# Two of six top-k selections moved behind the first blocks of the next attention head, with working tiles from that head's softmax ring

## The chip, the core and the metric

The kernel runs on one core of a Trainium2 chip. The metric is the device time of one execution in microseconds (us), the median of three runs where a median is given. The engines are called PE (matrix multiply, with PEld for its weight loads), DVE (the vector engine), ACT (the scalar engine), POOL (GpSimd) and SP, whose queue issues most of the DMA transfers. PSUM is the memory into which PE writes; a PSUM bank here holds a tile of 128x512 float32.

## What is computed

One decoder block on a sequence of 1024 rows and 1024 columns. After a projection, two attentions run side by side: eight "FoX" heads with a forget-gate bias, and eight "DSA" heads which see, for each query row, only the 256 keys with the highest indexer score, with a relative-position bias. The core of the second:

```python
iscore = jnp.where(causal[None], iscore, -jnp.inf)
_, sel = lax.top_k(iscore, topk)          # 256 of the keys s <= t
...
logits = logits + bias                     # relative-position bias
p = jax.nn.softmax(logits, axis=-1)
```

Gates, an output projection, a squared-ReLU MLP and a final norm follow. All matrix products are made from a high and a low part of each operand, three products for one.

## The kernel before

Rows are worked on in eight tiles of 128 query rows (i = 0 to 7). Row tile i sees (i + 1) * 128 keys, so the later tiles are the wider ones. Tiles 0 and 1 need no top-k.

**Selection.** The indexer scores of the tiles 2 to 7 stand in `isc` as sortable integers. A bisection over 32 bits (`bisect_step`, four steps for each FoX head) finds the threshold of each row. Then `select_tile(i)` (L521 to L535) makes the mask of tile i: nine DVE operations over (i + 1) * 128 columns and a read-back of one sum. They use two working tiles, `bjunk` (named gt) and `eqt` (named eq), of which there is one each, read `isc[i]`, and write the mask over `sel[i]`. The six calls stand at the end of the last FoX head's turn (L749 to L751).

**Attention.** `attention(kind, h, ...)` (L538) runs through four blocks qb = 0 to 3 of two row tiles each. For each row tile PE makes the scores S in PSUM (three banks go round, tag "S"), DVE adds the relative bias where there is one (L562) and adds the mask, taking the row minimum, into a softmax tile `sp` (L563), ACT makes the exponential (L567) and scales it (L570). Then PE transposes both tiles (L583), ACT and DVE split the transposes into `ph` and `pl` (L584, L585), and PE multiplies with V (pv). `sp` tiles come from a ring of four (tag "sp", bufs 4), two for each block. A DSA head's row tile i reads `sel[i]` from i = 2 on, so tiles 6 and 7 are read first in block qb = 3.

**Work beside it.** After each head's attention the program states the projection of the next head (`proj_qk`: two halves, each 24 matmuls of 128x512 into a PSUM bank of tag "g", of which there are two, emptied by ACT at L313 to L324 and by DVE at L318 and L325), for every second head `proj_v` (L338, L343, L344), gate tiles (`gate_tile`: two halves into the same "g" banks, emptied by ACT at L609), and, from the last FoX head on, `ada_later`, a chain of products on POOL (L618 to L627). These are PE's cover while the softmax chain of a head is under way.

**What sets the order.** The order on each engine is not the program's. A scheduler goes through a simulated timeline: an engine that is free takes, of the instructions whose inputs are there, the one that is stated first in the program. Rings of tiles go round in the order in which the program asks for tiles. On the chip every engine then goes through its list in that order, and waits where an input is late.

SP issues the loads for `branch_fox`, which go into the memory of `isc` (L649) after its last reader.

Of the kernel before, what the change touches and what calls it, by code (L numbers as in the profile page):

```python
# [11 lines left out]
BF16 = mybir.dt.bfloat16  # L12
# [9 lines left out]
P = 128  # L22
D = 1024
S = 1024
KT = D // P
NTT = S // P
# [31 lines left out]
def block_kernel(ctx: ExitStack, tc: tile.TileContext, x, c, w_ada, b_ada, g_norm1, w_in, b_forget,  # L58
# [5 lines left out]
    def pool(stack, name, bufs=1, **kw):  # L64
        if kw.get("space") != DRAM:
            kw.setdefault("reuse_waits", "tile")
        return stack.enter_context(tc.tile_pool(name=name, bufs=bufs, **kw))
# [260 lines left out]
    def proj_v(kind, pr):  # L328
        cv = (C_VF if kind == 0 else C_VD) + pr * P
        hi, lo = split_w([(0, P, win[:, :, cv:cv + P])], nc.gpsimd)  # L330
        V = [pQ.tile([P, NTT, P], F32R, name="V", tag="V", bufs=3) for _ in range(2)]
        for half in range(2):
            ps = gemm_h(hi, lo, half)
            vT = pQ.tile([P, 512], F32, name="t512", tag="t512", bufs=3)
            nc.scalar.activation(vT, ps, AF.Copy)
            tp = ptr.tile([P, 512], F32, name="vtr", tag="tr")
            for t in range(4):
                nc.tensor.transpose(tp[:, t * P:(t + 1) * P], vT[:, t * P:(t + 1) * P], ident)  # L338
            tv = tp.rearrange("p (t c) -> p t c", t=4)
            ts4 = slice(half * 4, half * 4 + 4)  # L340
            for s in range(2):
                src = tv[:, :, 64 * s:64 * s + 64]
                nc.scalar.activation(V[s][:, ts4, 0:64], src, AF.Copy)  # L343
                nc.vector.tensor_tensor(V[s][:, ts4, 64:128], src, V[s][:, ts4, 0:64].bitcast(F32), op=ALU.subtract)  # L344
        return V
# [114 lines left out]
    pA = pool(at_stack, "pA")  # L460
# [8 lines left out]
    bjunk = pA.tile([P, S], BF16, name="bjunk")  # L469
    eqt = pA.tile([P, S], BF16, name="eqt")  # L470
# [30 lines left out]
    def bisect_mid():  # L501
        nc.vector.tensor_scalar(cand, Thi, 1.0, None, op0=ALU.add)
        count(I16, cand)
        nc.vector.tensor_scalar(need, cnt, -1.0, float(TOPK), op0=ALU.mult, op1=ALU.add)
        for i in on_act:
            q = slice(i - 2, i - 1)
            nc.vector.tensor_scalar(need[:, q], cnt[:, q], -0.5, float(TOPK - (i + 1) * P // 2), op0=ALU.mult, op1=ALU.add)
        set_goal()
        for i in range(2, NTT):
            nc.vector.scalar_tensor_tensor(sel[i].bitcast(U16), sel[i].bitcast(I16), Thi[:, i - 2:i - 1],  # L510
                                           isc[i].bitcast(U16)[:, 0::2], op0=ALU.is_equal, op1=ALU.mult)
# [6 lines left out]
        nc.vector.tensor_tensor(cnt, cnt, goal, op=ALU.is_ge)  # L518
        nc.vector.scalar_tensor_tensor(T, cnt, v, T, op0=ALU.mult, op1=ALU.add)

    def select_tile(i):  # L521
        q, W = i - 2, (i + 1) * P
        hi = isc[i].bitcast(I16)[:, 1::2]
        L = sel[i].bitcast(U16)
        th, tl, nd = Thi[:, q:q + 1], Tlo[:, q:q + 1], need[:, q:q + 1]
        gt, eq = bjunk[:, :W], eqt[:, :W]
        nc.vector.tensor_scalar(gt, L, tl, None, op0=ALU.is_gt, op1=ALU.add, accum_out=cnt[:, q:q + 1])
        nc.vector.tensor_tensor(nd, nd, cnt[:, q:q + 1], op=ALU.subtract)
        nc.vector.tensor_scalar(eq, L, tl, None, op0=ALU.is_equal)
        nc.vector.scalar_tensor_tensor(gt, hi, th, gt, op0=ALU.is_gt, op1=ALU.add)  # L530
        nc.vector.scalar_tensor_tensor(eq, hi, th, eq, op0=ALU.is_equal, op1=ALU.mult)
        nc.vector.tensor_tensor_scan(out=L, data0=eq, data1=eq, initial=0.0, op0=ALU.add, op1=ALU.max)
        nc.vector.scalar_tensor_tensor(eq, L, nd, eq, op0=ALU.is_le, op1=ALU.mult)
        nc.vector.tensor_tensor(gt, gt, eq, op=ALU.add)
        nc.vector.tensor_scalar(sel[i], gt, -BIG, BIG, op0=ALU.mult, op1=ALU.add)  # L535


    def attention(kind, h, qk, V, Yd=None):  # L538
# [6 lines left out]
        for qb in range(NTT // 2):  # L545
            pt = []
            for s in range(2):
                i = 2 * qb + s
                W = (i + 1) * P
                qs = slice(i * P, (i + 1) * P)  # L550
                mn = pA.tile([P, 8], F32, name="mn", tag="mn", bufs=5)
                sp = pA.tile([P, S], F32, name="sp", tag="sp", bufs=4)
# [38 lines left out]
            nc.scalar.activation(yt, pv[64:128, :], AF.Copy)  # L591
            nc.vector.tensor_tensor(yt, pv[0:64, :], yt, op=ALU.add)  # L592
            nc.scalar.activation(yh, yt, AF.Copy)
            if (kind, h) == (1, NH - 1):
                cols = slice(qb * 256, (qb + 1) * 256)
                nc.scalar.activation(Yd[0][yr, 3, cols], yt, AF.Copy)
                nc.vector.tensor_tensor(Yd[1][yr, 3, cols], yt, yh.bitcast(F32), op=ALU.subtract)
                continue
# [4 lines left out]
    def gate_tile(g):  # L603
        col = (C_GF if g < 8 else C_GD) + (g % 8) * P
        hi, lo = split_w([(0, P, win[:, :, col:col + P])], nc.gpsimd)
        for half in range(2):
            ps = gemm_h(hi, lo, half)
            e = pQ.tile([P, 512], F32, name="t512", tag="t512", bufs=3)
            nc.scalar.activation(e, ps, AF.Tanh, scale=0.5)  # L609
            nc.sync.dma_start(G_d[g, :, half * 512:half * 512 + 512], e)  # L610
# [118 lines left out]
    for n, (kind, h) in enumerate(heads):  # L729
        qk = qk_next  # L730
        on_pool[0] = n < NH
        if h % 2 == 0:
            V = V_next
        attention(kind, h, qk, V[h % 2], Yd)
        if n + 1 < len(heads):
            qk_next = proj_qk(*heads[n + 1])
        if h % 2 == 1 and n + 1 < len(heads):
            V_next = proj_v(heads[n + 1][0], heads[n + 1][1] // 2)
        for g in GATES.get(n, ()):
            gate_tile(g)  # L740
        if n < NH:
            for b in range(4):
                if bit == 15:
                    bisect_mid()
                bisect_step(bit)
                bit -= 1
        if NH <= n + 1 < 2 * NH:
            ada_later(n + 1 - NH)
        if n == NH - 1:  # L749
            for i in range(2, NTT):  # L750
                select_tile(i)  # L751
        if n == 3:
            dsa_consts()
        for piece in PIECES.get(n, ()):
            branch_fox(piece)
        if n == 2 * NH - 2:
            h_stack.close()
            pYd = pool(yd_stack, "pYd", side="right")
            Yd = [pYd.tile([P, 4, S], F32R, name=f"Yd{v}") for v in range(2)]
            pY = pool(yd_stack, "pY", side="right")  # L760
# [14 lines left out]
    for half in range(2):  # L775
        sl = slice(half * 512, half * 512 + 512)
        for cp in range(4):
            hi, lo = split_w([(0, 256, wbv[1][:, :, cp * 256:cp * 256 + 256])], nc.gpsimd, 4)
            hv, lv = hi.rearrange("p (k c) -> p k c", k=4), lo.rearrange("p (k c) -> p k c", k=4)
            for c2 in range(2):  # L780
                ct, cs = 2 * cp + c2, slice(c2 * P, c2 * P + P)
                gt = pY.tile([P, 512], F32, name="gt2", tag="gt2", bufs=3)
# [432 lines left out]
```

## Time and profile before

| | us |
|---|---|
| median of three runs | 1624.54 |
| lowest and highest of them | 1622.43, 1626.76 |
| time of the profiled execution | 1624.31 |
| its span, first to last instruction | 1622.4 |
| PE busy | 1561.0 |
| DVE busy | 1142.8 |
| ACT busy | 946.8 |
| POOL busy | 742.1 |

The profiled execution stands 0.2 us under the median, and 1.9 us of its time lie outside the span. PE is busy for 96% of the span, so a change matters where it changes the idle time of PE, or the speed at which PE is clocked. The bisection ends at about 428 us, FoX head 6 runs to about 484, FoX head 7 from there to about 530 and the first DSA head from 514 to about 565; the heads overlap.

### The profile page before, as it was taken

The numbers are of one execution on the slowest core, as the hardware profiler recorded it, in microseconds if no ns is written. First come the engines' busy times: TensorE is split into PE (matmuls) and PEld (weight loads), VectorE is DVE, ScalarE is ACT, GpSimd is POOL, SyncE is SP. The second block draws the span as 40 slices with busy tenths as digits, with TensorE's granted clock in tenths as the row PEclk, the third lists the DMA queues.
The fourth block names the chain that finished last, engine by engine and source line by source line (L and its number), as shares of the span: only waits on it lengthen the run. The fifth ranks groups of instructions, "written<-read, shape, count | busy, mean of one in ns | idle before, by whom it ended". The sixth has DMA issues, their size and how long they took to land.

```text
span 1622.4 us, 22879 instructions
## 1 busy us (share of the span) xinstructions
PE 1561.0 (96%) x7585; PEld 1297.5 (80%) x7585; DVE 1142.8 (70%) x2230; ACT 946.8 (58%) x1689; POOL 742.1 (46%) x628
## 2 busy tenths in 40 slices
PE   5989999999989999999999998999999999999998
PEld 3767788887778888888887887888888878888887
DVE  6887778878897655557667546765655556668987
ACT  4455899898747767577763136554545543534433
POOL 3432222333234674756645211777776544334730
PEclk7999999999999999999999999999999999999999
DMA  9222122132124443544888456454444479755862
GB/s 307 78 47 60 52 80 57 44 79 50 53 63 140 119 139 99 153 135 138 300 262 272 144 164 225 150 161 162 149 147 160 164 263 388 244 201 199 280 208 104
DMA packets 223869, 253.01 MB, mean 156 GB/s; under 512 B 49136, under 2 KB 136256, under 8 KB 223752
## 3 DMA queue, kind: packets, MB, share of 16 engines
q1 hardware_dynamic: 215112, 233.73, 45.8%
q10 hardware_dynamic: 8640, 17.83, 2.9%
q8 instruction: 60, 0.98, 0.2%
q14 instruction: 57, 0.47, 0.1%
HBM read 186.48 MB, written 65.03 MB: 155 GB/s over the span
## 4 chain that ended last, share of the span: by engine, by line
PE 69%; DVE 10%; ACT 9%; issue 4%; DMA 4%; POOL 2%; SPq 1%; ACTq 0%; DVEq 0%; POOLq 0%
PE g L75 29%; PE S L75 23%; PE tr L75 8%; PE pv L75 7%; ACT eqt L495 4%; PE ptr L583 2%; DVE acc L252 2%; ACT sp L567 1%; ACT sp L570 1%; ACT ph L584 1%; DMA wap<-in_w_ada_dram 1%; DVE pl L585 1%; DMA gt<-G_d 1%; DVE sp L563 1%; DVE isc L434 1%
## 5 line engine op out<-in xcount | busy, mean ns | idle before, releaser
L75 PE MATMUL g<-h_hi,whi 128*128 128x512 f32 x656 | 263.8, 402 | 9.8 <-DVE KA L325 7.0
L75 PE MATMUL g<-h_hi,wlo 128*128 128x512 f32 x656 | 262.5, 400 | 0.0
L75 PE MATMUL g<-h_lo,whi 128*128 128x512 f32 x656 | 262.1, 399 | 0.0
L1036 DVE TENSOR_TENSOR big<-rw,big 128x1024 fp32r<-128x1024 f32 x112 | 174.7, 1605 | 76.7 <-ACT big L1035 76.7
L123 POOL TENSOR_TENSOR wlo<-st,whi 128x1024 fp32r<-128x1024 f32 x60 | 149.0, 2485 | 114.2 <-ACT whi L122 107.2
L1035 ACT ACTIVATE big<-rw 128x1024 fp32r<-128x1024 f32 x112 | 112.5, 1052 | 146.9 <-PE pv L75 63.2
L1051 POOL TENSOR_TENSOR rw<-rw 128x1024 f32<-128x1024 f32 x40 | 114.5, 2866 | 121.4 <-DMA rw<-in_w_mlp_dram 103.7
L75 PEld LDWEIGHTS g<-h_hi,whi 128*128 128x128 f32 x656 | 124.8, 190 | 35.5 <-issue 7.1
L75 PEld LDWEIGHTS g<-h_hi,wlo 128*128 128x128 f32 x656 | 124.4, 190 | 24.3
L75 PEld LDWEIGHTS g<-h_lo,whi 128*128 128x128 f32 x656 | 124.5, 190 | 22.7
L75 PE MATMUL S<-big 128*128 128x512 f32 (+1 forms) x576 | 136.5, 380 | 1.3 <-ACT big L1035 1.3
L75 PEld LDWEIGHTS S<-big 128*128 128x128 f32 x576 | 105.2, 188 | 22.3 <-ACT big L1035 1.7
L585 DVE TENSOR_TENSOR pl<-ptr,ph 128x512 fp32r<-128x512 f32 (+1 forms) x160 | 99.7, 631 | 23.7 <-ACT ph L584 20.6
L567 ACT ACTIVATE sp<-sp,mn 128x128 f32<-128x128 f32 (+7 forms) x128 | 98.5, 771 | 27.5 <-DVE mn L563 27.2
L584 ACT ACTIVATE ph<-ptr 128x512 fp32r<-128x512 f32 (+1 forms) x160 | 86.4, 550 | 43.6 <-PE ptr L583 41.7
L495 ACT ACTIVATE eqt<-sel_all,nct 128x768 bf16<-128x768 int16 (+5 forms) x99 | 102.5, 1035 | 10.0 <-DVE nct L491 8.7
L570 ACT ACTIVATE sp<-sp,mn 128x128 f32<-128x128 f32 (+7 forms) x128 | 96.9, 769 | 17.1 <-DVE mn L569 16.5
L75 PE MATMUL g<-big 128*128 128x512 f32 (+1 forms) x384 | 92.7, 376 | 0.0
L583 PE MATMUL ptr<-ident,sp 128*128 128x128 f32 x576 | 89.8, 272 | 1.7 <-DVE nct L491 1.2
L122 ACT ACTIVATE whi<-st 128x1024 fp32r<-128x1024 f32 x51 | 53.8, 1055 | 61.9 <-DMA st<-in_w_mlp_dram 19.4
L75 PE MATMUL pv<-ph,V 128*128 128x256 f32 x320 | 85.4, 286 | 3.1 <-DVE yt L592 3.1
L75 PE MATMUL pv<-pl,V 128*128 128x256 f32 x320 | 82.4, 285 | 2.8 <-DVE pl L585 1.6
(436 smaller groups left out, 3907.5 us busy)
## 6 DMA issues: line engine op xcount, KB each, us to landing
rw<-in_w_mlp_dram SPq DMA_DIRECT2D x72, 512.0 KB
rw<-U_d SPq DMA_DIRECT2D x56, 512.0 KB
wap<-in_w_ada_dram SPq DMA_DIRECT2D x64, 256.0 KB
st<-in_w_mlp_dram SPq DMA_DIRECT2D x32, 512.0 KB
st<-in_w_in_dram SPq DMA_DIRECT2D x26, 512.0 KB
U_d<-cc SPq DMA_DIRECT2D x48, 256.0 KB
st<-in_w_in_dram SPq DMA_DIRECT2D x33, 256.0 KB
G_d<-t SPq DMA_DIRECT2D x32, 256.0 KB
```

Source lines behind the costliest of these rows:

```text
L75: nc.tensor.matmul(o, l, r, start=start, stop=stop)
L122: nc.scalar.activation(hi, st, AF.Copy)
L123: (lo_eng or nc.vector).tensor_tensor(lo, st, hi.bitcast(F32), op=ALU.subtract)
L495: nc.scalar.activation(eqt[:, :(i + 1) * P], sel[i].bitcast(dt), AF.Sign, bias=nct[:, q], accum_out=cnt[:, q])
L567: nc.scalar.activation(sp[:, :W], sp[:, :W], AF.Exp, bias=mn[:, len(cs) - 1:len(cs)], scale=-1.0, accum_out=mn[:, 2:3])
L570: nc.scalar.activation(sp[:, :W], sp[:, :W], AF.Copy, scale=mn[:, 3:4])
L583: nc.tensor.transpose(tr[:, n * P:(n + 1) * P], pt[s][:, kb * P:(kb + 1) * P], ident)
L584: nc.scalar.activation(ph[:, z:], tr[:, z:], AF.Copy)
L585: nc.vector.tensor_tensor(pl[:, z:], tr[:, z:], ph[:, z:].bitcast(F32), op=ALU.subtract)
L1035: nc.scalar.activation(hl[:, 0], t, AF.Copy)
L1036: nc.vector.tensor_tensor(hl[:, 1], t, hl[:, 0].bitcast(F32), op=ALU.subtract)
L1051: nc.gpsimd.tensor_tensor(o, a, b, op=op)
```

## The change

`select_tile` takes an optional tile `room`, whose two halves replace `bjunk` and `eqt`. The calls for i = 6 and i = 7, the two widest, leave the last FoX head's turn. They are made inside the attention of the first DSA head (kind 1, h 0), after block qb = 0 (i = 6) and after block qb = 1 (i = 7), each with a `room` tile of the tag "sp", so that it takes one place of the ring of four.

```diff
-    def select_tile(i):
+    def select_tile(i, room=None):
...
-        gt, eq = bjunk[:, :W], eqt[:, :W]
+        gt, eq = (bjunk[:, :W], eqt[:, :W]) if room is None else (room[:, :W], room[:, S:S + W])
...
             nc.scalar.activation(yh, yt, AF.Copy)
+            if (kind, h) == (1, 0) and qb < 2:
+                room = pA.tile([P, 2 * S], BF16, name="room", tag="sp", bufs=4)
+                select_tile(6 + qb, room)
...
-            for i in range(2, NTT):
+            for i in range(2, 6):
                 select_tile(i)
```

## Rows read from the trace of the kernel before

**Rows 1.** Windows of 10 us: length, busy by engine (instructions), PE clock, DMA.

```profile
470.00:480.00 10.00, 7.05 (x23) 5.20 (x23) 9.94 (x14) 4.28 (x9) 8.05 (x5) 0.83 0.03 7
490.00:500.00 10.00, 10.00 (x57) 8.56 (x56) 9.96 (x15) 5.18 (x11) 3.43 (x5) 1.00 0.62 200
...
530.00:540.00 10.00, 10.00 (x55) 8.56 (x54) 5.39 (x15) 6.12 (x15) 4.57 (x8) 1.00 0.66 170
540.00:550.00 10.00, 10.00 (x55) 8.40 (x54) 6.27 (x20) 6.83 (x13) 6.03 (x6) 1.00 0.26 79
```

**Rows 2.** Timeline of PE: start, duration, instruction [idle before, releaser].

```profile
445.74 0.47 PE L75 MATMUL g<-h_hi,whi 128*128 128x512 f32 x1 [2.60 <-DVE KA L325]
...
473.21 0.35 PE L75 MATMUL pv<-ph,V 128*128 128x256 f32 x1 [1.61 <-DVE yt L592]
474.90 0.51 PE L75 MATMUL g<-h_hi,whi 128*128 128x512 f32 x1 [1.34 <-DVE KA L325]
475.25 0.40 PE L75 MATMUL g<-h_lo,whi 128*128 128x512 f32 x1
475.48 0.59 PE L75 MATMUL g<-h_hi,wlo 128*128 128x512 f32 x1
...
478.85 0.43 PE L75 MATMUL g<-h_lo,whi 128*128 128x512 f32 x1
```

**Rows 3.** Timeline of DVE, end of tile 6 and tile 7's selection.

```profile
483.11 0.39 DVE L535 TENSOR_SCALAR sel_all<-bjunk 128x896 bf16<-128x896 bf16 x1
483.42 0.48 DVE L529 TENSOR_SCALAR eqt<-sel_all,Tlo 128x1024 bf16<-128x1024 uint16 x1
...
484.49 1.28 DVE L527 TENSOR_SCALAR_CACHE_REDUCE bjunk<-sel_all,Tlo 128x1024 bf16<-128x1024 uint16 x1
...
489.35 2.27 DVE L532 TENSOR_TENSOR_SCAN sel_all<-eqt 128x1024 uint16<-128x1024 bf16 x1
...
493.79 0.67 DVE L534 TENSOR_TENSOR bjunk<-bjunk,eqt 128x1024 bf16<-128x1024 bf16 x1
...
495.32 3.19 DVE L535 TENSOR_SCALAR sel_all<-bjunk 128x1024 bf16<-128x1024 bf16 x1
```

**Rows 4.** Timeline of ACT at the two stalls of PE.

```profile
470.43 0.38 ACT L591 ACTIVATE yt<-pv 64x256 f32<-64x256 f32 x1
470.84 0.60 ACT L320 ACTIVATE KA<-g 64x512 fp32r<-64x512 f32 x1
```

**Rows 5.** Timeline of DVE, then PE: the ring of softmax tiles, first DSA head.

```profile
530.06 0.56 DVE L563 CUSTOM_DVE_ANT_0 sp<-S,sel_all 128x384 f32<-128x384 f32 x1 [0.32 <-PE ptr L583]
...
541.21 0.56 DVE L563 CUSTOM_DVE_ANT_0 sp<-S,sel_all 128x384 f32<-128x384 f32 x1 [3.09 <-PE ptr L583]
...
548.00 0.69 DVE L563 CUSTOM_DVE_ANT_0 sp<-S,sel_all 128x512 f32<-128x512 f32 x1 [0.25 <-PE ptr L583]
...
540.79 0.49 PE L583 MATMUL ptr<-ident,sp 128*128 128x128 f32 x3
```

**Rows 6.** Timelines of ACT, DVE, PE: the banks of PE's cover, same head.

```profile
529.65 0.60 ACT L324 ACTIVATE KB<-g 64x512 fp32r<-64x512 f32 x1
...
531.27 0.69 DVE L325 TENSOR_TENSOR KA<-g,KA 64x512 fp32r<-64x512 f32 x1
...
535.18 0.39 PE L75 MATMUL g<-h_hi,whi 128*128 128x512 f32 x1
...
553.18 0.59 ACT L313 ACTIVATE QA<-g 64x512 fp32r<-64x512 f32 x1 [0.85 <-PE S L75]
```

**Rows 7.** Windows of 30 us, columns as Rows 1; then one POOL instruction.

```profile
469.00:499.00 30.00, 27.05 (x132) 22.55 (x133) 29.77 (x45) 13.55 (x28) 12.61 (x13) 0.94 0.30 82
520.00:550.00 30.00, 30.00 (x168) 25.84 (x167) 17.78 (x46) 20.98 (x45) 19.37 (x21) 1.00 0.49 138
...
494.80 2.85 POOL L123 TENSOR_TENSOR wlo<-st,whi 128x1024 fp32r<-128x1024 f32 x1 [5.17 <-DMA isc<-Y_d]
```

**Rows 8.** Waits of SP's queue, 425 to 600 us: total, times, longest.

```profile
SPq L649 <- DVE mn L569: 7.6, 1, 7.6
```

## The prediction

> **What bounds the kernel now.** I read the page's busy times first (the table above): PE is by far the busiest, so only its idle time and its clock can give anything back. Next come the windows over the stretch that the change touches [rows 1]. Between 470 and 480 us PE is busy for 7.05 of 10 us, at a mean granted clock of 0.83, and DVE is full (9.94). Between 490 and 500 DVE is still full, and PE is full as well: there PE has other work. From 530 to 550, in the first DSA head, PE is full and DVE has 4.6 and 3.7 us free in 10.
>
> The timeline of PE names what it waits for [rows 2]. Two waits lie where tiles 6 and 7 are selected: 1.61 us for yt (L592) and 1.34 us for KA (L325), both on DVE. After them comes a slow piece: eight matmuls from 475.48 to 478.85 take 3.37 us, 0.42 each, while the pair from 475.25 to 475.48 is 0.23 apart. PE had stood still for most of the 3.5 us ahead of 474.90, and then ran at the lower of its two levels (1.2 instead of 2.4 GHz). The earlier wait of 2.60 us at 445.74 belongs to the tiles before tile 6, which stay where they are and are ordered before anything that moves, so it stays.
>
> **What the change removes.** *The work.* Tile 7's selection [rows 3]: L529 0.48, then four operations over 1024 columns of about 1.28 each (L527 stands for them, the others are L530, L531, L533), the scan 2.27, L534 0.67, L535 3.19. Two short ones are left out. L535 of tile 6, over 896 columns, took 0.39, so 0.45 would be its due for 1024 and 2.74 of the 3.19 is something else (below). Clean, tile 7 is 0.48 + 5.12 + 2.27 + 0.67 + 0.45 = 9.0 us, and tile 6 at seven eighths of the width 7.9 us: about 17 us of DVE leave the stretch from 469 to 499.
>
> *What that gives PE.* Only the two waits and the slow piece, since after 479 PE is full with or without it. When tile 6 is gone, ACT is late next [rows 4]: its half of yt ends at 470.81, so DVE's 0.42 could end near 471.2, and the 1.61 go entirely. KA's first half ends on ACT at 471.44; DVE's 0.69 would end near 472.2, where it now ends near 474.9. PE would then stand for some 0.6 us instead of 2.95, a gain of 2.35. The slow piece would be eight times 0.23 = 1.84 instead of 3.37: 1.5 more. Sum 3.9 us. The ends are nothing (another late input in the same place) and 2.95 + 1.5 = 4.5.
>
> **What it adds.** *The place.* Rings go round in order of the program. The ring of four softmax tiles shows it: row tile 2 starts at 530.06, 0.32 us after DVE began to wait for the transposes that free the place of FoX head 7's tile 6, and row tile 4 waits 3.09 us for the transposes of 540.79, which free the place of row tile 0 [rows 5]. With the change the place freed at about 530 goes to tile 6's room, row tile 2 takes the other place freed there, and row tile 3 has to wait for 540.8 to 541.2 (it could start straight behind row tile 2 before). Tile 7's room comes free at the same 541.2. So selection of tile 6 starts near 530 and of tile 7 near 541, both inside the DSA head.
>
> *Its rank.* Where it stood, selection was stated last, and DVE took it up only when nothing else was there. Now it is stated ahead of blocks 1 to 3 and of the next head's projection, so it goes before those whenever both are ready.
>
> *Tile 6 and the bank.* L325, which empties a "g" bank, becomes ready when ACT ends at 530.25 and runs at 531.27 [rows 6]; the next group of 24 matmuls starts at 535.18 in that bank. L325 is stated after the attention, so tile 6's chain ranks ahead of it. If the chain starts first, L325 is queued behind 7.9 us of selection and what else DVE has there that ranks higher: its 5.39 us of work from 530 to 540 [rows 1], less L325 itself and row tile 3, of 0.69 each like the 512 columns of [rows 5], 4.0 us. From 529.9 that is 541.8, so L325 ends near 542.5 instead of 532, and PE's next group starts 7.3 us late. Other PE work in that time is about 1.5 us (a few pv, transposes and scores). That makes a stall of 5.8 us, and 1.5 to 1.9 of slow matmuls after it, as in [rows 2]. If L325 slips in between, it costs nothing; there is no reason for a gain, since PE is full there [rows 1]. The two become ready within 0.4 us of each other, so I take half of 5.8: 2.9.
>
> *Tile 7 and the head's end.* Its 9.0 us from 541.2, with up to 6.27 us of other work of DVE in such a stretch [rows 1], push row tiles 4 to 6 back: L563 of row tile 6 at 548.00 [rows 5] goes to about 556.5, and the last scores of row tile 7, for which ACT waits at 553.18 [rows 6], go to about 558, 5 us late. The cover is the second half of the next projection, 24 x 0.23 = 5.5 us, for which one bank is free. So 0 to 3, and I take 0.6. If that cover is gone, the whole 5 shows.
>
> *SP's queue.* The loads into `isc` wait for selection's last reader; before, SP stood 7.6 us for that and everything behind it stood too [rows 8]. That wait moves to about 550. What is queued there is stores and prefetches with several us in hand. I take nothing, up to 2 for a late weight load, and the same in the other direction where it stood.
>
> *POOL.* L535's 3.19 us starts at 495.32 while a POOL operation runs from 494.80 to 497.65 [rows 3, 7], and it ends 0.86 us after it: DVE was held, in part at least, by POOL. POOL is busy for 12.61 of 30 us where selection stood and 19.37 of 30 where it goes [rows 7]. The Trainium skill, page "SBUF — State Buffer", section "SBUF: two separate sides", says that GpSimd and certain DVE operations (those that use two ports, or have two SBUF inputs) share a port pair as an exclusive lock, so that the later one blocks for the whole of the other's instruction. By that rule the hold would grow with POOL's share. It speaks against the new place. The row's own 2.74 us times 19.37 / 12.61 is 4.2, so 1.5 us more of DVE time; it is a rival below and not in the sum.
>
> **The sum**, against the profiled execution's own 1624.3 (0.2 below the median): 1624.3 - 3.9 + 2.9 + 0.6 = 1623.9, say 1624.
>
> **Rivals.** *Clean gain.* DVE's free 4.6 and 3.7 us in 10 [rows 1], and the softmax chain of head 7 running ahead once DVE is relieved, swallow both selections: 1624.3 - 3.9 = 1620.4, and up to 3 us less if the waits further on fall better. For it speaks that PE is full in all three of the later windows [rows 1]; against it, that selection needs 17 us in some 25 that have about 10 free.
>
> *The bank is held (slower).* The chain takes DVE before L325 and keeps PE out of the bank: 1624.3 - 3.9 + 5.8 + 1.7 + 3 = 1631. It decides from the point where L325 ends later than about 533, plus PE's 1.5 us of other work. The 2.60 us at 445.74 [rows 2] are just this wait, with selection ranking last; against it stands only the near tie.
>
> *POOL holds selection.* A DVE operation that starts under a POOL operation waits for its end. With POOL busy for two thirds of the time, 1.5 us more lie on the same bank: 1624 + 1.5 = 1625.5. The long L535 (3.19 against 0.39 [rows 3]) speaks for it, and that POOL's `ada_later` is made of short operations speaks against.
>
> *It doesn't move.* If rooms were handed out whenever a place is free, selection would start near its old time, and take softmax places there: 1624, within 1.
>
> **How the numbers follow.** A measurement of this kernel can tell about 0.3%, 4.9 us, from no change: the bounds are 1619.7 and 1629.4. Chances: forecast (1621 to 1627) 0.42, clean gain (1616 to 1621) 0.22, bank held (1627 to 1633) 0.20, POOL 0.09, no move 0.07. Of the clean gain the greater part passes the lower bound only if something further on falls well too, of the held bank most passes the upper one. Faster: 0.18 from the clean gain and 0.02 of the forecast's tail, 0.20. Slower: 0.19 of the held bank, 0.03 of POOL's and 0.03 of the forecast's tail, 0.25. Within: 0.55. The range runs from 1617 to 1632, which leaves out about 1 in 10 at each end.
>
> **What would show it.** Right: the two waits of 473.21 and 474.90 and the slow piece are gone; L527 over 896 columns starts right after the last transposes of FoX head 7, and over 1024 columns after those of block 0; a PE wait for L325 of 1 to 6 us stands beside tile 6's chain. Wrong: no PE wait in the first DSA head (clean gain), a second low-clock piece there (bank held), L535 or L533 of several us (POOL), or a room that starts before FoX head 7 has ended. The prediction fails outright if order elsewhere shifts by more than the 4.9 us, which no row here can exclude.

## The result

The change makes the kernel slower: 1640.68 us median (1639.45 to 1641.71) beside 1625.65 us (1622.43 to 1627.15) for the kernel before, a ratio of 1.0092 (95% interval 1.0079 to 1.0104). The forecast was 1624 with a range of 1617 to 1632. The profiled execution took 1641.4 us, its span is 1638.9 us.

To see where the time went, take the matmuls in the order in which they start, give each the duration of its shape, and ask when each kernel has reached the same sum. Up to about 430 us the instructions of all kernels stand in the same order, and their executions still differ by 1 to 5 us, from a start that varies. So the table gives first how far each kernel already lags (+) at 428 us, and then what it loses (+) or gains (-) in each stretch against the kernel before. The names are those of the experiments below. Where the order is that of the kernel before, stretches still differ by 1 to 2 us (late_order in 428-521, before_dve in 665-772), which is the table's own scatter.

```
us lost against before; stretch ends are times of the kernel before
                 lag  428-521 521-562 562-665 665-772 772-856 856-1008
changed         +2.5    -4.3   +10.2    -0.3    -2.3    +6.5    +4.1
only6           +1.1    +1.6    +3.5    +0.2    -3.8    +4.6    +6.3
only7           +4.3    +0.8    +7.3    +0.1    -3.8    +2.9    +4.8
leaveout        +1.4    -2.9    +0.3    -0.3    -3.3    +2.0    +2.6
placeonly       +2.7    -5.4    +0.2     0.0    -4.0    +3.2    +3.1
oldring         +1.8    -4.7   +14.3    +0.3    -1.1    +4.6    +3.5
short7          +1.6    -4.3    +1.2    +0.1    -1.3    +4.1    +5.1
late_order      +1.2    -1.1     0.0     0.0    -4.0    +5.1    +2.9
before_q        +2.3    -1.2     0.0     0.0    +0.8    +1.4    +6.0
after_q         +4.6    -4.3   +10.1    -0.3    -2.3    +5.6    +6.1
before_deep     +1.7    -0.1     0.0     0.0    -1.4    -1.7    +1.5
after_deep      +2.3    -5.9    +9.6    -0.2    -3.8    -0.8    +7.5
late_deep       +1.9    +0.2     0.0     0.0    -3.7    -0.3    +6.2
after_deepdve   +0.9    -4.3   +10.2    -0.2    -3.8    -1.1    +7.6
late_deepdve    +2.2    -0.8     0.0     0.0    -3.7    -1.8    +6.4
before_dve      +3.7    +0.3     0.0     0.0    -2.0    +1.0    +0.2
before_deepdve  +1.2    -1.1     0.0     0.0    -0.2    -1.5    -1.5
```

For the changed kernel: 4.3 us gained where selection was, 10.2 lost where it went, 2.6 gained from 562 to 772 us, and 10.6 lost after that, in stages that the change does not touch. The sum of the stretches is 13.9, near the 15.0 between the medians.

**The gain came.** Windows of 10 us of the changed kernel: busy time by engine, clock, DMA. Against [rows 1], the slow clock at 470 us is gone, and DVE, full before, has 2.7 and 5.8 us free at 470 and 490:

```profile
470.00:480.00 10.00, 8.23 (x44) 6.68 (x44) 7.28 (x18) 6.70 (x12) 4.29 (x8) 1.00 0.09 23
490.00:500.00 10.00, 10.00 (x58) 8.66 (x58) 4.15 (x15) 6.41 (x14) 5.79 (x9) 1.00 0.27 81
...
530.00:540.00 10.00, 9.48 (x49) 7.76 (x48) 9.94 (x18) 5.26 (x12) 0.00 (x0) 1.00 0.36 87
540.00:550.00 10.00, 9.58 (x49) 7.78 (x48) 9.96 (x18) 4.22 (x9) 2.70 (x3) 1.00 0.35 100
550.00:560.00 10.00, 8.86 (x47) 7.00 (x46) 9.10 (x23) 5.82 (x10) 0.40 (x1) 1.00 0.69 221
560.00:570.00 10.00, 6.34 (x22) 5.03 (x23) 7.11 (x19) 9.81 (x18) 7.15 (x9) 0.66 0.55 131
```

The same rows show the price. DVE is full from 530 to 550 (9.94, 9.96) where it was busy for 5.39 and 6.27, and PE is busy for only 6.34 of 10 us from 560, at a mean clock of 0.66.

**The waits.** The changed kernel's PE timeline (start, duration, instruction, idle before and releaser). The waits of 1.61 and 1.34 us [rows 2] have become 0.29; a wait just ahead of them, for a softmax row minimum, has grown from 1.03 us to 1.48. Tile 6 costs 0.52 for the bank; behind tile 7 come 0.42 and then three longer waits in a row:

```profile
471.84 0.44 PE L75 MATMUL S<-KA,QA 128*128 128x384 f32 x1 [1.48 <-DVE mn L563]
474.83 0.47 PE L75 MATMUL g<-h_hi,whi 128*128 128x512 f32 x1 [0.29 <-DVE KA L325]
...
534.55 0.50 PE L75 MATMUL g<-h_hi,whi 128*128 128x512 f32 x1 [0.52 <-DVE KA L325]
549.01 0.50 PE L75 MATMUL S<-KA,QA 128*128 128x512 f32 x1 [0.42 <-DVE mn L563]
558.63 0.88 PE L583 MATMUL ptr<-ident,sp 128*128 128x128 f32 x6 [1.12 <-ACT sp L570]
562.12 0.44 PE L75 MATMUL S<-KA,QA 128*128 128x384 f32 x1 [2.14 <-DVE mn L563]
564.06 0.58 PE L75 MATMUL pv<-ph,V 128*128 128x256 f32 x1 [1.32 <-ACT ph L584]
```

The DVE timeline of the changed kernel shows both tiles where the ring was expected to put them, L527 of tile 6 at 526.58 and of tile 7 at 541.40. It also shows two of their operations beside a POOL operation (third fence from here). L325 slips into tile 6's chain at 533.80. L563 at 554.80 belongs to row tile 6; the last one, of row tile 7, ends at 562.1:

```profile
526.58 1.15 DVE L527 TENSOR_SCALAR_CACHE_REDUCE room<-sel_all,Tlo 128x896 bf16<-128x896 uint16 x1 [1.01 <-PE ptr L583]
527.65 2.32 DVE L529 TENSOR_SCALAR room<-sel_all,Tlo 128x896 bf16<-128x896 uint16 x1
...
530.97 0.14 DVE L528 TENSOR_TENSOR need<-need,cnt 128x1 f32<-128x1 f32 x1
...
533.80 0.69 DVE L325 TENSOR_TENSOR KA<-g,KA 64x512 fp32r<-64x512 f32 x1
...
541.40 1.28 DVE L527 TENSOR_SCALAR_CACHE_REDUCE room<-sel_all,Tlo 128x1024 bf16<-128x1024 uint16 x1
...
544.01 2.16 DVE L528 TENSOR_TENSOR need<-need,cnt 128x1 f32<-128x1 f32 x1
...
554.80 0.67 DVE L563 CUSTOM_DVE_ANT_0 sp<-S,sel_all 128x512 f32<-128x512 f32 x1
...
556.61 0.41 DVE L535 TENSOR_SCALAR sel_all<-room 128x1024 bf16<-128x1024 bf16 x1
...
561.33 0.73 DVE L563 CUSTOM_DVE_ANT_0 sp<-S,sel_all,mn 128x512 f32<-128x512 f32 x1
```

In the kernel before the last one ends at 554.6 (DVE):

```profile
553.89 0.75 DVE L563 CUSTOM_DVE_ANT_0 sp<-S,sel_all,mn 128x512 f32<-128x512 f32 x1
```

POOL of the changed kernel at the two slow operations:

```profile
527.32 2.40 POOL L123 TENSOR_TENSOR wlo<-st,whi 128x1024 fp32r<-128x1024 f32 x1
...
543.74 2.41 POOL L123 TENSOR_TENSOR wlo<-st,whi 128x1024 fp32r<-128x1024 f32 x1 [14.02 <-ACT whi L122]
```

ACT, where it empties both halves of the next projection (these rows are used further on):

```profile
560.98 0.59 ACT L313 ACTIVATE QA<-g 64x512 fp32r<-64x512 f32 x1
...
562.19 0.59 ACT L313 ACTIVATE QA<-g 64x512 fp32r<-64x512 f32 x1
```

**Later.** PE of the changed kernel after 690 us, its waits of over 1 us:

```profile
704.83 0.50 PE L75 MATMUL g<-h_hi,whi 128*128 128x512 f32 x1 [1.37 <-DVE t L671]
...
791.06 0.54 PE L75 MATMUL g<-h_hi,whi 128*128 128x512 f32 x1 [2.62 <-DVE t L671]
...
880.34 1.22 PE L75 MATMUL S<-Yd,whi 128*128 128x512 f32 x2 [2.74 <-DVE gt L792]
903.38 0.70 PE L75 MATMUL S<-Yd,whi 128*128 128x512 f32 x2 [1.28 <-DVE gt L792]
```

The kernel before has only two of this kind (L668 and L789 are the same lines there):

```profile
686.81 0.54 PE L75 MATMUL g<-h_hi,whi 128*128 128x512 f32 x1 [1.77 <-DVE t L668]
...
872.51 0.50 PE L75 MATMUL S<-Yd,whi 128*128 128x512 f32 x1 [0.73 <-DVE gt L789]
```

All are for a DVE operation that multiplies a gate into a product. At the four of the changed kernel DVE in turn waits for the gate's load (three of the four are shown; the fourth is like the third), and at the first two SP's queue, which issues it, has been waiting itself (DVE timeline, then SP's waits from 690 to 710 us and from 768 to 792 us: total, times, longest):

```profile
704.09 0.69 DVE L671 SCALAR_TENSOR_TENSOR t<-t,g 128x512 f32<-128x512 f32 x1 [5.98 <-DMA t<-G_d]
...
790.31 0.69 DVE L671 SCALAR_TENSOR_TENSOR t<-t,g 128x512 f32<-128x512 f32 x1 [3.24 <-DMA t<-G_d]
...
879.60 0.69 DVE L792 SCALAR_TENSOR_TENSOR gt<-gt,S 128x512 f32<-128x512 f32 x1 [4.93 <-DMA gt<-G_d]
```
```profile
SPq L667 <- DMA M_d<-t: 2.9, 1, 2.9
...
SPq L114 <- POOL wlo L123: 4.5, 1, 4.5
SPq L672 <- DVE mn L569: 3.4, 1, 3.4
SPq L667 <- DMA M_d<-t: 3.3, 1, 3.3
```

The row `L667 <- DMA M_d<-t` says that a gate's load waits until an earlier tile of its ring of three has been stored. The other two rows, for POOL and for DVE, show waits as long on the same queue.

### The profile page after: what moved, and what is told of

It reads as the page before. It is cut to its first block, busy times and chain, and to the rows that moved or that the text cites. A ratio compares the mean times of both kernels' runs of the same rounds, so it can differ in the third digit from the quotient of the medians.

```text
span 1638.9 us, 22875 instructions
## 1 busy us (share of the span) xinstructions
PE 1567.0 (96%) x7585; PEld 1300.6 (79%) x7585; DVE 1137.9 (69%) x2230; ACT 948.1 (58%) x1689; POOL 736.0 (45%) x628
## 4 chain that ended last, share of the span: by engine, by line
PE 68%; DVE 12%; ACT 9%; DMA 4%; issue 3%; POOL 2%; SPq 1%; ACTq 0%; DVEq 0%; POOLq 0%
PE g L75 28%; PE S L75 22%; PE tr L75 8%; PE pv L75 6%; ACT eqt L495 4%; PE ptr L583 2%; ACT sp L567 1%; DVE acc L252 1%; ACT sp L570 1%; DVE sp L563 1%; DMA gt<-G_d 1%; DVE pl L585 1%; ACT ph L584 1%; DMA t<-G_d 1%; DVE isc L434 1%
## 5 line engine op out<-in xcount | busy, mean ns | idle before, releaser
L75 PE MATMUL g<-h_hi,whi 128*128 128x512 f32 x656 | 264.2, 403 | 10.6 <-DVE KA L325 5.9
L123 POOL TENSOR_TENSOR wlo<-st,whi 128x1024 fp32r<-128x1024 f32 x60 | 145.6, 2428 | 139.4 <-ACT whi L122 124.4
L584 ACT ACTIVATE ph<-ptr 128x512 fp32r<-128x512 f32 (+1 forms) x160 | 86.1, 551 | 51.1 <-PE ptr L583 46.4
```

The costliest lines, as they stand in the source:

```text
L75: nc.tensor.matmul(o, l, r, start=start, stop=stop)
L123: (lo_eng or nc.vector).tensor_tensor(lo, st, hi.bitcast(F32), op=ALU.subtract)
L584: nc.scalar.activation(ph[:, z:], tr[:, z:], AF.Copy)
```

## The experiments

Each ratio is to runs of the kernel before that were taken with it.

**One tile at a time.** only6 and only7 hold back one tile and leave the other in its old place.

```diff
-            if (kind, h) == (1, 0) and qb < 2:
+            if (kind, h) == (1, 0) and qb == 0:      # only6; only7: qb == 1
...
-            for i in range(2, 6):
+            for i in (2, 3, 4, 5, 7):                # only7: range(2, 7)
```

> Only the selection of row tile 6 is held back; tile 7 is selected in its old place. Theory: local loss about 1 us (as measured at 530 to 540 us of the changed kernel), gain about 2 us at 475 us, nothing lost from 541 to 570 us, and since nothing is late, nothing is lost after 640 us: 1622 to 1626 us. Rival (each shift of the program order, however small, reshuffles the later stages and costs some 8 us there): 1630 to 1634 us.

> Only the selection of row tile 7 is held back into the head; tile 6 is selected in its old place, after the eighth forget-gate head. Theory (the nine operations of tile 7 on VectorE push the scores of row tile 7 back by some 9 us): the +9.3 us that the changed kernel loses from 541 to 570 us stays whole, of the gain of 4.2 us at 475 us about half stays, and the loss after 640 us (+8 in the changed kernel), if it is a consequence of that delay, stays too: 1634 to 1640 us. Rival (two places of the softmax ring taken one after the other, or the sum of both tiles): under half of the 9.3 us stays, 1624 to 1630 us.

Measured: only6 1637.83 us, 1.0078 (1.0059 to 1.0097); only7 1638.86 us, 1.0088 (1.0066 to 1.0110). Only7's time is in the range of its theory, though the half of the gain that it was to keep is missing; only6 is above its theory and its rival. As a whole the parts do not add up: each alone costs almost as much as both. In the head they do, 3.5 and 7.3 us beside 10.2. The gain is whole or nothing. With either tile left in the old place, the two waits and the slow clock stay: in only7 tile 6 is still selected there, and in only6 tile 7 takes its place on DVE. PE of only7, then of only6:

```profile
477.44 0.35 PE L75 MATMUL pv<-ph,V 128*128 128x256 f32 x1 [1.61 <-DVE yt L592]
479.13 0.80 PE L75 MATMUL g<-h_hi,whi 128*128 128x512 f32 x1 [1.34 <-DVE KA L325]
```
```profile
474.49 0.36 PE L75 MATMUL pv<-ph,V 128*128 128x256 f32 x1 [1.44 <-DVE yt L592]
476.41 0.79 PE L75 MATMUL g<-h_hi,whi 128*128 128x512 f32 x1 [1.56 <-DVE KA L325]
```

In the head, tile 7 alone costs 7.3 us and tile 6 alone 3.5, of which 1 was expected. Only6 then loses 10.9 us after 772 us. It can't say whether that follows from the delay, since it leaves the head about as late as the changed kernel (5.3 and 5.6 us behind its own lag, at 665 us). The next two kernels can.

**No work, or no place.** leaveout copies both masks from the causal mask in the old place; placeonly takes the two places in the ring and copies the causal mask through them. In both, the selection of row tiles 6 and 7 is left out.

```diff
# leaveout, in the old place; the calls in the head are gone
...
+            for i in (6, 7):
+                nc.vector.tensor_copy(sel[i], cmask[:, S - (i + 1) * P:])
# placeonly, in the head
-                select_tile(6 + qb, room)
+                i = 6 + qb
+                nc.vector.tensor_copy(room[:, :(i + 1) * P], cmask[:, S - (i + 1) * P:])
+                nc.vector.tensor_copy(sel[i], room[:, :(i + 1) * P])
```

> Row tiles 6 and 7 are not selected at all: their masks are copied from the causal mask, by one operation each in the old place, so the output is another one. This is the gain without any cost. Theory: the 4.2 us at 475 us come, and with no selection in the head the loss from 541 to 570 us is gone, and the loss after 640 us with it: 1619 to 1622 us. Rival (the later stages lose because the order is another one): about 1628 us.

> As the changed kernel, with both places of the softmax ring taken in the head, but in place of the eighteen operations of the selection stand two copies for each tile (the causal mask into the place and from there into the tile's mask), so the output is another one. Theory (the work on VectorE costs, not the place): within 3 us of the kernel that leaves both out, 1619 to 1625 us. Rival (the place costs: row tiles wait for a softmax tile, the pipelining is halved): half or more of the 9.3 us from 541 to 570 us stays, 1626 to 1636 us.

Measured: leaveout 1623.52 us, 0.9991 (0.9981 to 1.0001); placeonly 1624.57 us, 1.0003 (0.9992 to 1.0014). Placeonly came as its theory said; leaveout lies above its theory (1619 to 1622) and below its rival. In the head they lose 0.3 and 0.2 us: the places cost nothing, the work costs. And even without any selection of the two tiles the kernel is not measurably faster, since what is gained up to 772 us (6.2 and 9.2) is mostly lost again after it (4.6 and 6.3). Both are ahead of the kernel before at 772 us, so the late loss doesn't need a delay in the head. A version without a place to wait for (working tiles `bjunk` and `eqt`, calls in the head) was not run; the scheduler gives all five engines exactly the order of the kernel before. So the ring decides when selection runs, and DVE's time what that costs.

**Another place, less work.** oldring keeps the ring but states both tiles in the old place of the program, so each waits for a softmax tile of the last FoX head. short7 is the changed kernel with tile 7 cut to L527, L529, L528 and L535; the rest of its selection is left out.

```diff
# oldring; the calls in the head are gone
...
-            for i in range(2, 6):
-                select_tile(i)
+            for i in range(2, NTT):
+                room = None
+                if i > 5:
+                    room = pA.tile([P, 2 * S], BF16, name="room", tag="sp", bufs=4)
+                select_tile(i, room)
# short7, in select_tile after the comparison of the low halves
+        if i == 7:
+            nc.vector.tensor_scalar(sel[i], gt, -BIG, BIG, op0=ALU.mult, op1=ALU.add)
+            return
```

> Tiles 6 and 7 take their working tiles from the softmax ring as in the changed kernel, but in the old place of the program, ahead of the first relative-bias head. So each waits for a place that a row tile of the last forget-gate head gives back, and should start near 505 us, some 20 us earlier than in the changed kernel. Theory (the place in the order decides: the operations of tile 7 in the middle of the head push its last row tile back): the gain of about 4 us near 475 us stays, of the 9.3 us lost from 541 to 570 us under 3 us stays, the stages after 640 us lose 2 to 10 us, as the order there is a new one again: 1622 to 1633 us. Rival (VectorE has no room between 500 and 560 us wherever the selection stands): the local loss stays, 1633 to 1640 us.

> The changed kernel with the selection of row tile 7 cut to four of its nine operations (the two comparisons of the low halves, the small subtraction, the mask), so its mask is another one. The five left out took 1.27, 1.27, 2.28, 1.26 and 0.68 us in the changed kernel, 6.8 us together; the place in the ring, the start and the rank of the tile stay, and the order of TensorE is the same up to there. Theory (what is lost is VectorE's time in front of the last row tile's scores, one for one beyond a fixed cover): of the 9.3 us lost from 541 to 570 us some 2 to 4 us stay. Rival (the tile's start in the middle of the head or its place in the ring costs, whatever it computes): 6 us or more stay. The total follows the late order, a new one again: 1626 to 1636 us.

Measured: oldring 1642.15 us, 1.0096 (1.0079 to 1.0114); short7 1631.74 us, 1.0051 (1.0033 to 1.0069). Short7 kept 1.2 us of the loss, less than the 2 to 4 of its theory, and its time is in the range. For oldring the expectation failed: it is above its theory and its rival. Its selection starts at 514.41, not near 505, its eighteen operations take 24 us of DVE up to 544, and PE stands and is then clocked lower (PE of oldring, then a window):

```profile
528.99 1.12 PE L583 MATMUL ptr<-ident,sp 128*128 128x128 f32 x4 [6.22 <-DVE pl L585]
533.20 0.80 PE L75 MATMUL g<-h_hi,whi 128*128 128x512 f32 x1 [3.09 <-DVE KA L325]
```
```profile
530.00:540.00 10.00, 6.91 (x20) 5.43 (x20) 9.94 (x10) 2.20 (x4) 0.82 (x3) 0.58 0.96 287
```

In short7, 6.8 us less of DVE's work bring back 9.0 of the 10.2 us, waits and slow clock together, though the place, the start and the hold of L528 by POOL (2.16 us again) stay. Windows of short7:

```profile
550.00:560.00 10.00, 9.71 (x58) 8.21 (x57) 8.25 (x24) 9.21 (x16) 5.09 (x7) 1.00 0.38 110
560.00:570.00 10.00, 10.00 (x51) 8.37 (x50) 4.60 (x11) 7.77 (x17) 8.38 (x7) 1.00 0.62 154
```

The kernels that select in the head give one rule. Take the start of the last L563 of row tile 7 (553.89 before) and subtract what the kernel already lags or leads at 521 us: this is how late the head's last scores are. In the four that select there the loss follows it about one for one, with little cover left over, and placeonly is the zero point:

```
              L563 at   lag at 521   late by   lost 521-562
changed        561.33      -1.8         9.2        10.2
only6          560.09      +2.7         3.5         3.5
only7          565.04      +5.1         6.1         7.3
short7         553.19      -2.7         2.0         1.2
placeonly      550.21      -2.7        -1.0         0.2
oldring        566.12      -2.9        15.1        14.3
```

Oldring, the last row, is no proof of it. About 12 of its 14.3 us are lost at the two waits above and at the lower clock up to 538 us, long before the last scores, which are late there because PE itself is. In the other kernels nearly all of the loss comes behind 556 us.

**The order alone.** late_order is the kernel before with two small copies (0.28 us each) in the third DSA head; from 626 us on, every engine has another order.

```diff
             nc.scalar.activation(yh, yt, AF.Copy)
+            if (kind, h) == (1, 2) and qb == 0:
+                for _ in range(2):
+                    nc.vector.tensor_copy(bjunk[0:64, 0:256], yt)
```

> The kernel before with two copies of 64x256 elements on VectorE added in the third relative-bias head (under 1 us of work). Up to there, about 620 us, the order of every engine is that of the kernel before; behind it the order is another one on all five. Theory (the loss after 640 us comes from the new order of the loads on the SP queue, not from the delay in the first head): no loss before 620 us, 3 to 10 us lost after it: 1627 to 1634 us. Rival (the loss after 640 us is a consequence of the delay in the head): 1624 to 1626 us.

Measured: 1631.57 us, 1.0037 (1.0024 to 1.0050), as its theory said. Nothing is lost up to 665 us, 4.0 us are gained up to 772 and 8.0 lost up to 1008, so the stages after the head lose by a new order alone. PE of late_order waits as the changed kernel does:

```profile
780.08 0.50 PE L75 MATMUL g<-h_hi,whi 128*128 128x512 f32 x1 [1.77 <-DVE t L671]
801.84 0.73 PE L75 MATMUL g<-isc,whi 128*128 128x512 f32 x2 [1.45 <-DVE t L671]
```

**Another queue.** before_q and after_q issue the loads of the gates and of the first branch's result from ACT.

```diff
-            nc.sync.dma_start(g, G_d[ct, :, sl])
+            nc.scalar.dma_start(g, G_d[ct, :, sl])
...
-                nc.sync.dma_start(gt, G_d[8 + ct, :, sl])
-                nc.sync.dma_start(mf, M_d[ct, :, sl])
+                nc.scalar.dma_start(gt, G_d[8 + ct, :, sl])
+                nc.scalar.dma_start(mf, M_d[ct, :, sl])
```

> The kernel before with the loads of the gates and of the first branch's result (the 16 of the first branch, the 32 of the second stage) issued on ScalarE's queue in place of SP's. The kernel before waits only 1.8 and 0.7 us for these loads. Theory: 1621 to 1626 us. Rival (issuing costs ScalarE, or stalls it behind a full ring): 1627 us or more.

> The changed kernel with the same loads on ScalarE's queue; the order up to about 760 us is that of the changed kernel. Theory (these loads stand behind other transfers and their waits on the SP queue, and TensorE's waits of 2.62, 2.74 and 1.28 us come from that): of the 10 us lost after 690 us at least half goes, 1630 to 1636 us. Rival (the loads come late because the transfers themselves are late or slow, or the operations behind them): 1638 to 1642 us.

Measured: before_q 1635.76 us, 1.0060 (1.0043 to 1.0077); after_q 1640.81 us, 1.0092 (1.0070 to 1.0115). Both are in the ranges of their rivals: the loss stays, and the kernel before gets slower. In after_q the wait of 2.62 us is gone, and PE waits 2.48 us for ACT's `ph` (L584) at 814 us instead; whether the loads on ACT's queue cause that is not shown.

**Deeper rings.** In before_deep and after_deep every second gate tile of the first branch comes from the bisection's two scratch tiles, and the second stage's gates and results have four places each. late_deep is late_order with these and a third place for the accumulators (`aca`, the sums of `ada_later`, loaded for the second stage).

```diff
-    bjunk = pA.tile([P, S], BF16, name="bjunk")
-    eqt = pA.tile([P, S], BF16, name="eqt")
+    bjunk = pA.tile([P, S], BF16, name="bjunk", tag="bj", bufs=2)
+    eqt = pA.tile([P, S], BF16, name="eqt", tag="bj", bufs=2)
...
-            g = pQ.tile([P, 512], F32, name="t512", tag="t512", bufs=3)
+            if ct % 2:
+                g = pA.tile([P, 512], F32, name="g5", tag="bj", bufs=2)
+            else:
+                g = pQ.tile([P, 512], F32, name="t512", tag="t512", bufs=3)
...
-                gt = pY.tile([P, 512], F32, name="gt2", tag="gt2", bufs=3)
-                mf = pY.tile([P, 512], F32, name="mf", tag="mf", bufs=3)
+                gt = pY.tile([P, 512], F32, name="gt2", tag="gt2", bufs=4)
+                mf = pY.tile([P, 512], F32, name="mf", tag="mf", bufs=4)
```

> The kernel before with more room for the late loads: the gate tiles of the first branch come alternately from their ring of three and from the two scratch tiles of the bisection, which are free by then (five in all), and the rings of gates and of first-branch results in the second stage have four places instead of three. Theory (loads come late because each waits until an earlier tile of its ring is stored, so that any order with the load a little later on the SP queue makes TensorE wait): the waits of 1.77 us at 687 us and 0.73 us at 873 us go, with the slower clock behind the first: 1617 to 1623 us. Rival (the load's place on the SP queue decides, the depth of the ring does not): 1624 to 1632 us, a new order costing what it costs elsewhere.

> The changed kernel with the same deeper rings; up to about 690 us its order is that of the changed kernel, so the local gain of 4 us and loss of 10 us stay. Theory: of the 10 us that the changed kernel loses after 690 us at least half goes, 1629 to 1635 us. Rival (the place on the queue decides): 1637 to 1643 us.

> The kernel of the run late_order (kernel before and two small copies in the third relative-bias head) with the deeper rings of before_deep and a third place for the accumulators of the adaptive rows. Without the rings it gained 2.4 and 1.3 us at 590 and 620 us and lost 8.7 us from 690 to 800 us. Theory (the rings are too shallow to hide a load that stands later on the queue): under 3 us of the 8.7 stay, and the gain stays: 1618 to 1624 us, at or below the kernel before. Rival (the place on the queue decides): 1626 to 1634 us.

Measured: before_deep 1623.93 us, 0.9988 (0.9979 to 0.9998); after_deep 1633.53 us, 1.0049 (1.0031 to 1.0067); late_deep 1628.64 us, 1.0029 (1.0018 to 1.0039). Only after_deep is in the range of its theory; before_deep misses it by 0.9 us, and the wait at 687 us that it was to remove is still there (2.04 us, last fence here). In the stretch of the first branch, 772 to 856 us, the ring decides. The eight kernels with three places, their loads on SP, and a new order from the first or third DSA head on lose 2.0 to 6.5 us there, and in each PE waits for the first branch's product (the line of L671) 1.3 to 2.6 us at once; all six with five places have no such wait there and lose nothing (-0.3 to -1.8). late_deep as a whole missed its expectation, since the loss comes back one stage later: 6.2 us after 856 us, and 7.5 in after_deep. PE of after_deep, then of before_deep:

```profile
873.31 1.84 PE L75 MATMUL tr<-onesf,aca 128*128 128x1 f32 x8 [3.59 <-DMA aca<-A_d]
876.63 1.22 PE L75 MATMUL S<-Yd,whi 128*128 128x512 f32 x2 [1.49 <-DVE gt L795]
```
```profile
688.69 0.50 PE L75 MATMUL g<-h_hi,whi 128*128 128x512 f32 x1 [2.04 <-DVE t L671]
```

**POOL or the queue.** Beside those waits DVE of after_deep takes 5.51 us for two operations that take 0.68 each elsewhere, next to two of POOL (DVE, then POOL). Late_deep has the same (5.51 beside 5.39), and there PE waits 2.44 us for that line at 869.84:

```profile
870.41 5.51 DVE L799 SCALAR_TENSOR_TENSOR big<-gt,big 128x512 fp32r<-128x512 f32 x2
```
```profile
869.95 5.41 POOL L732 TENSOR_TENSOR wol<-st,woh 128x1024 fp32r<-128x1024 f32 x2 [0.69 <-ACT woh L731]
```

The last four kernels put the sixteen splits of the second stage and of the output weights on DVE, on top of the kernel before, of before_deep and after_deep, and of late_deep without its third place.

```diff
-            hi, lo = split_w([(0, 256, wbv[1][:, :, cp * 256:cp * 256 + 256])], nc.gpsimd, 4)
+            hi, lo = split_w([(0, 256, wbv[1][:, :, cp * 256:cp * 256 + 256])], None, 4)
...
-        nc.gpsimd.tensor_tensor(lo, sv, hi.bitcast(F32), op=ALU.subtract)
+        nc.vector.tensor_tensor(lo, sv, hi.bitcast(F32), op=ALU.subtract)
```

> The kernel of the run after_deep with the sixteen low-half splits of the second stage and of the output weights (128x1024 each) on VectorE in place of GpSimd; up to about 830 us its order is that of after_deep. Theory (GpSimd's splits of some 2.5 us each hold VectorE, and with it the loads that wait for VectorE's last reader): of the 8 us that after_deep loses against the kernel before from 860 to 905 us at least half goes, 1626 to 1630 us. Rival (the load of the accumulators stands too late on the SP queue): 1632 to 1636 us.

> late_deep with the same sixteen splits on VectorE (and two places for the accumulators, as in the kernel before). Theory: of the 6.6 us that late_deep loses at 860 to 880 us at least half goes: 1620 to 1625 us. Rival: 1627 to 1631 us.

> The kernel before with the same sixteen splits on VectorE. It loses only 0.73 us and a little slow clock from 860 to 905 us, so there is little to gain; VectorE gets 16 operations of some 1.3 us more, in stretches where it is busy for 4 to 9 of 10 us. Theory: 1621 to 1625 us. Rival (VectorE becomes the later one in the second stage): 1627 us or more.

> before_deep with the same sixteen splits on VectorE. Theory: before_deep's waits of 0.59 and 0.92 us at 883 and 886 us go: 1619 to 1623 us. Rival (VectorE becomes the later one): 1626 us or more.

Measured: after_deepdve 1633.29 us, 1.0052 (1.0033 to 1.0071); late_deepdve 1628.72 us, 1.0029 (1.0018 to 1.0041); before_dve 1626.35 us, 1.0014 (1.0004 to 1.0023); before_deepdve 1621.51 us, 0.9982 (0.9972 to 0.9991). Before_deepdve is in the range of its theory, the other three are not. Against after_deep, after_deepdve changes the splits alone, and the theory falls: POOL is idle from 860 to 880 us and 7.6 us are lost all the same. In late_deepdve, also with POOL idle, it is 6.4. In both the accumulators' load is late, and the clock falls with the waits. PE of after_deepdve, and its window from 870:

```profile
871.71 3.57 PE L75 MATMUL tr<-onesf,aca 128*128 128x1 f32 x16 [2.16 <-DMA aca<-A_d]
```
```profile
870.00:880.00 10.00, 7.43 (x25) 6.57 (x26) 7.67 (x13) 3.24 (x5) 0.00 (x0) 0.57 0.84 280
```

Late_deepdve went back to two places for the accumulators, and no run has the third place together with the splits on DVE, nor an earlier load. So it stays open what of the loss after 856 us is the load, what POOL, and what the new order around them. Without any change ahead of 688 us, deeper rings and splits on DVE together gain 2 us on the kernel before. That is the fastest of the kernels, though within the 0.3% that the prediction called the same.

## Why the prediction was wrong

**The gain was right.** The terms were 2.35 for the waits and 1.5 for the slow piece, 3.9 together; 4.3 was measured, and 4.3 to 5.9 in the five other kernels that have this order up to 521 us. KA was the input that is late next, with 0.29 us left of 1.34.

**Where and when was right.** Rooms came free where the ring of [rows 5] puts them, at 526.6 (3.4 us ahead of the forecast 530) and 541.4. "It doesn't move" is out, and so is a cost of the place itself (placeonly).

**Tile 6's bank was near its lower end.** The tie between L325 and the chain went the cheap way: L325 ran at 533.80, and the wait is 0.52 us, where 2.9 was put between 0 and 5.8. The rival in which the bank is held did not happen here, though its 1631 lies nearest to the result; in oldring a wait of 3.09 us for L325 stands.

**The step that failed in the head is "Tile 7 and the head's end".** The delay was put at 5 us and was 9.2; the cover was put at 5.5 us and was none; the term was 0.6 us, and 10.2 were lost in the head. On the delay: the prediction put row tile 6 at 556.5, 8.5 us late, and the last scores at 558, only 5 late, as if row tiles caught up on the way. Measured, L563 of row tile 6 starts at 554.80, 6.8 late, and the last one 7.4 late: nothing is caught up. On top, the kernel leads by 1.8 us at 521 us, and loses that in the same place; the prediction had booked the gain and then counted the head from unmoved times. It also charged tile 6 to the bank alone, while only6 is 3.5 us late at the head's end with tile 6 alone and loses as much there. The cover is no cover, since the projection's 24 matmuls of 5.5 us are work that PE does in any case. While row tiles 4 to 6 were late, PE did them ahead of time: between 556 and 564 us it has no projection matmul left, and at 560.98 and 562.19 ACT takes both halves of QA out of their banks (L313), where [rows 6] has the first at 553.18. Work done early fills a hole only if it is not needed later, at the end. The prediction had named the case ("if that cover is gone, the whole 5 shows") and left it outside its bounds of 0 to 3; the table of late scores shows that it is the rule in these kernels.

**The step that failed after the head is "SP's queue", put at nothing, up to 2.** It looked at the wait that moves [rows 8] and not at the order. The edits in one head gave the engines another order for all that follows, and the kernel before has one in which gates with three places arrive almost in time (its waits are 1.77 and 0.73 us). Each of the eight new orders with three places lost 4.6 to 10.9 us from 772 to 1008 us, late_order too, whose head is untouched, and leaveout, which removes work. Of the changed kernel's 10.6 us there, 6.5 lie in the first branch, where five places take the loss away; the cause of the other 4.1 stays open. The prediction's last sentence named this as what would make it fail outright; it should have been a rival with a price and a chance.

**POOL.** The rival's mechanism was right: 1.9 us on L529 of tile 6 (0.43 before) and 2.0 on L528 of tile 7, 3.9 together, where 4.2 was worked out from POOL's share. That the size agrees is luck: the 4.2 came from POOL being busy for 19.37 of 30 us, and in the changed kernel it is busy for 11.76 of the same 30, with two operations of 2.4 us that happen to meet selection. The two tiles take about 10.1 and 11.2 us of DVE instead of 7.9 and 9.0. What of the 9.2 us of delay these holds make is not shown, since no run takes POOL out of the head. L528 handles 128x1 elements and takes 0.14 us alone, but 2.16 beside POOL's 2.41; it ends with POOL's operation. With that, the rule that the prediction cites from the Trainium skill ("SBUF — State Buffer", section "SBUF: two separate sides"), by which the later of the two blocks for the whole of the other's instruction, agrees with this trace.

## What to carry to other kernels

Before moving work off a busy engine, ask which stretch of the bottleneck lives off that engine: here the old place cost 4 us because TensorE had projections of its own beside it, and the new one cost what it delayed, about one for one. Work that the bottleneck can do early is cover only once, and the end of a head needs it. Where a program's order comes from a scheduler, a small edit can give everything behind it another order: price that as a case of its own by trivial edits. One or two places more for loads that arrive just in time took the loss away in one stage here, and not in the next.

## What the runs showed of the hardware

A DVE operation of 128x1 elements took 2.16 us instead of 0.14 beside one POOL operation, and two of 128x512 took 5.51 instead of 1.36 beside two of POOL's. TensorE's granted clock fell once more behind short waits: waits of 1.12 and 2.14 us end at 558.63 and 562.12, the mean from 560 to 570 us is 0.66, and matmuls run at 1.2 instead of 2.4 GHz from 564 to 569 us; 256 columns then lie 0.21 us apart, where they lay 0.12 apart at 556 us. From 564.06 to 569.45 PE does in 5.4 us what takes about 2.4 at the pace of 0.23 us for 512 columns, 0.21 of it a wait, so the slow piece is at most about 2.8 of the 10.2 us that the head lost.
